# Attention with a bias on one core: pair 0's bias chunk moved, and pair 1's first head copied straight from PSUM

## The chip, the core and the metric

The kernel runs on one core of a Trainium2 chip. A core has five engines that run side by side, each with its own list of instructions in a fixed order: TensorE (PE: matmuls, and PEld: its weight loads), VectorE (DVE), ScalarE (ACT), GpSimd (POOL) and SyncE (SP). They wait for one another by semaphores. SP, ScalarE and POOL can issue DMA transfers; the transfers run on 16 shared DMA engines. The metric is the device time of one execution in microseconds (us); lower is better.

## The reference

Batch 4, 8 heads, sequence 1024, head size 64, all float32; the bias is one 1024x1024 matrix that all 32 heads share.

```python
scores = scale * np.matmul(q, k.transpose(0, 1, 3, 2))
scores = scores + bias
scores_max = np.max(scores, axis=-1, keepdims=True)
attn = np.exp(scores - scores_max) / (np.sum(np.exp(scores - scores_max), axis=-1, keepdims=True) + 1e-8)
return np.matmul(attn, v).astype(np.float32)
```

## The kernel before

Two heads make a pair; there are 16 pairs. The queries are cut into 8 chunks of 128. A **slot** is one chunk of one head: its scores against all 1024 keys, 128x1024 in float32, which is one of three PSUM places (`places`, each of two banks). There are 256 slots. Each is filled by PE (`fill`, 8 matmuls of 128 columns), turned into exp by ScalarE (`exp`, line 258, 128x1024 in one instruction) or, for 19 planned slots, by six steps on DVE, and then multiplied with v (`av`, line 312, 8 matmuls of 65 columns; the last column sums the row). DVE divides (`evac`) and SP stores.

The bias is not added anew for each head. A place starts with the bias by a matmul of the bias chunk with a scaled identity (`"b"`, line 241) and the scores of the first head on top (`"s"`, line 244). From then on the place keeps its PSUM: the next head's fill adds (new scores minus old scores), from one matmul of depth 128 whose two halves are the new head's k and q and the old head's k and negated q. So of each pair four arrays are needed: `ko`, `qo` (both heads of the pair stacked; q with a sign) and `ke`, `qe` (the pair's first head in rows 0 to 63, and the pair before's second head in rows 64 to 127). `copy_out` (lines 199, 201) brings the transposed k or q from PSUM to `ko` or `qo`; `double` (lines 210, 212) copies a half of them on into a `ke` or `qe`. Slots 0, 1, 2 are head 0 on query chunks 0, 1, 2 in places 0, 1, 2; slots 3 to 5 are head 1 there; slots 6 to 8 are head 2, pair 1's first; slots 9 to 11 head 3, and so on.

The order on each engine is set when the kernel is built. The opening (lines 337 to 392) is written out by hand: q and k of pair 0 are loaded in float32 on SP's queue (`q0f`, `k0f`), the bias's chunk 0 (`b0f`) on ScalarE's, and all are cast to bfloat16 by DVE and ScalarE (lines 370 to 373); ten matmuls of zeros keep PE running (line 360); ScalarE loads its exp table (line 347). All later loads go through POOL's queue, which casts on the way: bias chunks 1 and 2, then k and q of pair 1 (of q three chunks), k and q of pair 2, v of pair 0, k of pair 3, and so on (lines 352 to 358, then `early`). Behind the opening a planner (lines 394 to 826) with fixed costs and landing times decides the order: it appends to each engine's list the work that is ready first by its own clock. PE's transposes of k and q for later pairs (line 191, from the bfloat16 loads) go to the PSUM banks `xa` and `xb`, which are also those of `av`; a bank is free again when its copy has been made.

Of the kernel before, what the change touches and what calls it, by code (L numbers as in the profile page):

```python
# [16 lines left out]
def kernel(  # L17
# [13 lines left out]
    nc = tc.nc  # L31
# [150 lines left out]
    def transposes(pr, which, c0, n, tag, px=None):  # L182
        if px is None:
            px = ps_x.tile([P, n, P], BF, tag=tag, name="px")
        for c in range(n):
            if (pr, which, c0) in raws:
                nc.tensor.transpose(px[:, c, :], raws[pr, which, c0][:, c].rearrange("p t d -> p (t d)"), ident[:])  # L187
                continue

            for t in range(2):  # L190
                nc.tensor.transpose(px[t * D:(t + 1) * D, c, :], lands[pr, which, c0][:, t, c, :], ident[:],  # L191
                                    tile_position=(0, t * D))
        return px

    def copy_out(pr, which, c0, n, px):
        t = arrays(pr)
        cs = slice(c0, c0 + n)
        if which:
            nc.vector.tensor_copy(t["ko"][:, cs, :], px[:])  # L199
        else:  # L200
            nc.vector.tensor_scalar(t["qo"][:, cs, :], px[:], sgn[:], None, op0=ALU.mult)  # L201

    def double(pr, which, c0, n, part, w):
# [7 lines left out]
        else:  # L211
            w.tensor_scalar(to[("qe", "qe", "qs", "qz")[part]][rows, cs, :], t["qo"][rows, cs, :], -1.0, 1.0,
                            op0=ALU.mult, op1=ALU.mult)

    def negate(pr):

        t = (raws[pr, 0, 0] if 0 in BESIDE else lands[pr, 0, 0]).rearrange("p t c d -> p (t c d)").rearrange("p (c x) -> p c x", x=P)
        nc.vector.tensor_scalar(t, arrs[pr]["qo"][:], -1.0, 1.0, op0=ALU.mult, op1=ALU.mult)
        return t
# [10 lines left out]
            return t["ko"], t["qz"] if pr in first_pair else t["qs"]  # L230
        return (t["ko"], t["qo"]) if h % 2 else (t["ke"], t["qe"])

    def fill_half(s, b, what):

        x, c, h, start = slots[s]
        kk, qq = operands(s)
        for i in range(4):
            kc = 4 * b + i
            to = places[x][:, b, i * P:(i + 1) * P]
            if what == "b":  # L240
                nc.tensor.matmul(to, braw[:, c, :].rearrange("p (kp kc) -> p kc kp", kc=NCH)[:, kc, :], ident8[:],  # L241
                                 start=i == 0, stop=False, skip_group_check=True)
            else:
                nc.tensor.matmul(to, kk[:, kc, :], qq[:, c, :], start=False, stop=True, skip_group_check=True)  # L244

    def fill(s):
        for what in "bs" if slots[s][3] and s > 1 else "s":
            for b in range(2):
                fill_half(s, b, what)

    etile = {}

    def exp(s, i=0, n=2):

        if i == 0:
            etile[s] = ep.tile([P, NCH, P], BF, name="E")
        e = etile[s].rearrange("p (b c) q -> p b (c q)", b=2)
        nc.scalar.activation(e[:, i:i + n].rearrange("p b x -> p (b x)"),  # L258
                             places[slots[s][0]][:, i:i + n].rearrange("p b x -> p (b x)"), ACTF.Exp, scale=scale)
# [75 lines left out]
    with tc.manual_schedule():  # L335

        half = NCH // 2
        nc.sync.dma_start(out=q0f[:], in_=qf[0][:, :, :C0 * D].rearrange("p t (c d) -> p t c d", d=D))
        nc.scalar.dma_start(out=b0f[:], in_=bf_[:, 0, :])
        for i in range(2):  # L340
            nc.sync.dma_start(out=k0f[:, :, i * half:(i + 1) * half].rearrange("p t c d -> p t (c d)"),
                              in_=kf[0][:, :, i * half * D:(i + 1) * half * D])
# [2 lines left out]
        nc.vector.memset(sgn[:D, :], -1.0)  # L345
        nc.vector.memset(sgn[D:, :], 1.0)
        nc.scalar.activation(warm[:], warm[:], ACTF.Exp)
        make_identity(nc, ident[:])

        nc.gpsimd.memset(qz[0][D:, :, :], 0.0)  # L350
# [5 lines left out]
        load_k(2)  # L356
        load_q(2, slice(0, NCH))
        load_v(0)
        for i in range(10):
            nc.tensor.matmul(places[2][:, 0, :], zeros[:, :P], zeros, start=True, stop=True)  # L360

        cast = [de.tile([P, NCH, P], BF, name="de").rearrange("p c (t d) -> p c t d", d=D) for i in range(2)]
        qr0 = raws[0, 0, 0] = cast[0][:, half:half + C0]
# [5 lines left out]
        nc.vector.tensor_scalar(ident8[:], ident[:], 1.0 / scale, None, op0=ALU.mult)  # L369
        nc.vector.tensor_copy(qr0.rearrange("p c t d -> p t c d"), q0f[:])  # L370
        nc.vector.tensor_copy(kr0[0].rearrange("p c t d -> p t c d"), k0f[:, :, :half])
        nc.scalar.copy(braw[:, 0, :], b0f[:])
        nc.scalar.copy(kr0[1].rearrange("p c t d -> p t c d"), k0f[:, :, half:])

        pq = transposes(0, 0, 0, C0, "xa")
        pk = transposes(0, 1, 0, half, "xb")
        pk2 = places[2].bitcast(BF)[:, 1, :half * P].rearrange("p (c x) -> p c x", x=P)
        nc.vector.tensor_scalar(t0["qz"][:D, :C0, :], pq[:D], 1.0, None, op0=ALU.mult)
        copy_out(0, 1, 0, half, pk)
        for i in range(2):  # L380
            fill_half(0, i, "b")
        transposes(0, 1, half, half, None, px=pk2)
        copy_out(0, 1, half, half, pk2)
        copy_out(0, 0, 0, C0, pq)
        fill_half(0, 0, "s")
        exp(0, 0, 1)
        for i in range(2):
            fill_half(1, i, "b")
        fill_half(0, 1, "s")
        exp(0, 1, 1)  # L390
        double(0, 1, 0, NCH, 1, nc.vector)
        double(0, 0, 0, C0, 1, nc.vector)

# [38 lines left out]
        TR, SWITCH = 56, 190  # L432
        LATE, QCOST = 2, 4400
        flight = []

        LATE_LOADS = {"v5": 34200, "q0": 37900, "v6": 41000, "q1": 43000, "b3": 35900, "b4": 39300, "b5": 44400,
                      "b6": 46100, "b7": 47800}
# [82 lines left out]
                issue(0, E2, depth, load_b, pr)  # L520
                bias_at[pr] = LATE_LOADS["b%d" % pr]

        def doubles(pr, which, c0, n, t2, urgent):
            if not which and pr >= EARLY:
                def run(t3):
                    to = negate(pr)
                    last = parts(pr, 0)[-1]
                    for x in parts(pr, 0):
                        key = (("qe", "qe1", "qs", "qz")[x], pr + (x == 1), 0)
                        sp_q.append((t3 + 430 + L_DVE, lambda t4, x=x, key=key: copy(pr, x, key[0][:2], to, key, t4, x == last)))  # L530
                dve_q.append((t2, 0.2 if urgent else 2, 430, run))
                return
            for x in parts(pr, which):
                key = (("ke", "ke1")[x], pr + (x == 1)) if which else (("qe", "qe1", "qs", "qz")[x], pr + (x == 1), c0)
                if which and (pr >= EARLY or x == 1 and pr >= 2):
                    sp_q.append((t2 + L_DVE, lambda t3, x=x, key=key: copy(pr, x, "ke", arrs[pr]["ko"], key, t3)))
                elif which or urgent:
                    cost = (130 if which else 240) + 38 * n

                    def run(t3, x=x, key=key, cost=cost):  # L540
                        double(pr, which, c0, n, x, nc.vector)
                        ready[key] = t3 + cost + L_DVE
                    dve_q.append((t2, (0.2, 0.4, 0.4, 0.2)[x] if urgent else 2, cost, run))
                else:
                    double(pr, which, c0, n, x, nc.gpsimd)
                    pool(t2)
                    ready[key] = pool(0, 125 * n + 100) + 300
# [40 lines left out]
        def pe_cands():  # L588
# [69 lines left out]
            if pieces:  # L658
                pr, which, c0, n = pieces[0]
                need = need_at[pr, which, c0]  # L660
                ring = pr + linked(pr) - RING
                lag = len([s for s in avq[:NE] if s in e_at])
                if ((pr, which, c0) in raw_at and next_fill >= need - AHEAD and (ring < 0 or last_slot[ring] < next_fill)
                        and (lag < 4 or need - next_fill < 8)):
                    f, tag = min((x_free[y], y) for y in x_free)
                    r = max(f, raw_at[pr, which, c0])
                    cost = n * TR + SWITCH * (pr < EARLY or which not in BESIDE)
                    urgent = need - next_fill < 12
                    if r < 1e11:
                        def do(t, pr=pr, which=which, c0=c0, n=n, tag=tag, cost=cost):  # L670
                            x_free[tag] = 1e12
                            pieces.pop(0)
                            px = transposes(pr, which, c0, n, tag)
                            if pr < EARLY and which == 0 and c0 == 0:
                                freed(pr, t)

                            def run(t2):
                                copy_out(pr, which, c0, n, px)
                                done = t2 + 60 * n + (180 if which else 300)
                                x_free[tag] = done + L_DVE  # L680
                                if which:
                                    ready["ko", pr] = done + L_DVE
                                else:
                                    ready["qo", pr, c0] = done + L_DVE
                                doubles(pr, which, c0, n, done, urgent)
                            dve_q.append((t + cost + L_PE, 0 if urgent else 2, 60 * n + (180 if which else 300), run))
                        out.append((max(t_pe, r), cost, do, 2 if next_fill < need - 12 else 0.5, 0))
            return out

# [167 lines left out]
```

## Time and profile before

| what | us |
|---|---|
| median of 3 runs | 232.8 (232.72 to 233.51) |
| the profiled execution | 232.74 |
| its span | 230.8 |
| PE busy | 222.9 (97%) |
| ACT busy | 221.3 (96%) |
| DVE busy | 197.0 (85%) |
| POOL busy | 63.4 (27%) |
| exps on ScalarE (line 258) | 238, 218.1 in total, 1.124 each |
| first exp starts | 8.04 |

Times in the profile are us from the span's start. Busy time of PE counts a matmul from its issue to its modelled end, and matmuls overlap: 8 matmuls of 128 columns follow each other every 0.056 or so and each takes 0.219. Likewise the exps on ScalarE take 1.0 to 1.1 each, and start about 0.9 apart. An idle time in brackets is that of the engine just before the row, with what ended it. The chain of work that ended last is followed back from the last instruction, at each step to what released it or to the instruction ahead of it on its engine.

### The profile page before, as it was taken

To read this page: it belongs to the slowest core of one execution; us is meant where nothing else is said; L and a number is where in the kernel's file an instruction comes from. 1 tells how busy PE (TensorE), PEld (TensorE's weight loads), DVE (VectorE), ACT (ScalarE), POOL (GpSimd) and SP (SyncE) were. 2 spreads that over 40 slices of the span, in tenths; PEclk is the share of its full clock that TensorE was granted. 3 is DMA by queue.
4 is the path that set the end of the run, shared out by engine and by line. 5 is a ranking of instruction groups with operands and counts; after the bars stand their busy time and mean duration, and the time that the engine had idled before them with its cause. 6 is when DMAs were issued, how large, how long until landed. Compare 5 with 4: busy or idle time off the path is not lost.

```text
span 230.8 us, 10694 instructions
## 1 busy us (share of the span) xinstructions
PE 222.9 (97%) x4671; PEld 209.9 (91%) x4671; DVE 197.0 (85%) x294; ACT 221.3 (96%) x242; POOL 63.4 (27%) x115
## 2 busy tenths in 40 slices
PE   7999999999999999999999999999999999999993
PEld 2879999999999999998999999999998999999992
DVE  3595768799988997989889789899999899999993
ACT  3799999999999999999999999999999999999994
POOL 8816555144445374414216310000000000000000
PEclk9999999999999999999999999999999999999999
DMA  6999999969999799999999993111111112112212
GB/s 198 214 205 225 215 206 183 216 96 151 154 172 130 153 164 158 170 171 185 176 214 191 196 191 107 43 37 43 40 39 47 45 43 65 53 26 66 71 31 68
DMA packets 55645, 29.75 MB, mean 129 GB/s; under 512 B 31856, under 2 KB 51952, under 8 KB 55600
## 3 DMA queue, kind: packets, MB, share of 16 engines
q0 software_dynamic: 30336, 14.06, 49.6%
q1 hardware_dynamic: 24832, 14.43, 21.8%
q8 instruction: 36, 0.59, 1.1%
q10 hardware_dynamic: 432, 0.59, 0.9%
q14 instruction: 9, 0.07, 0.1%
HBM read 29.36 MB, written 8.39 MB: 164 GB/s over the span
## 4 chain that ended last, share of the span: by engine, by line
PE 43%; ACT 28%; issue 13%; DVE 5%; DMA 5%; POOL 3%; SPq 1%; DVEq 0%; ACTq 0%; POOLq 0%
ACT E L258 28%; PE pl L244 25%; PE po L312 12%; DMA k<-in_k_dram 4%; PE px L191 4%; PE pl L241 2%; DVE ob L322 1%; DVE dt L290 1%; DVE dy L275 1%; DVE de L295 1%; SPq L706 1%; POOL k L145 1%; POOL q L155 1%; DMA out_dram<-ob 1%; PE px L187 1%
## 5 line engine op out<-in xcount | busy, mean ns | idle before, releaser
L258 ACT ACTIVATE E<-pl 128x1024 bf16<-128x1024 f32 (+1 forms) x238 | 218.1, 1124 | 1.9 <-PE pl L244 1.7
L312 PE MATMUL po<-vall,E 128*128 128x65 bf16 x1896 | 92.0, 194 | 0.7 <-ACT E L258 0.7
L312 PEld LDWEIGHTS <-E 128*128 128x128 bf16 x1896 | 77.5, 98 | 1.8 <-ACT E L258 1.1
L244 PE MATMUL pl<-qo,ko 128*128 128x128 bf16 x1024 | 77.0, 219 | 1.2 <-ACT E L258 0.7
L244 PEld LDWEIGHTS <-ko 128*128 128x128 bf16 x1160 | 69.6, 98 | 4.4 <-issue 1.2
L244 PE MATMUL pl<-qe,ke 128*128 128x128 bf16 x888 | 66.0, 219 | 0.6
L244 PEld LDWEIGHTS <-ke 128*128 128x128 bf16 x888 | 53.4, 98 | 3.3
L275 DVE TENSOR_SCALAR dy<-pl 128x1024 int32<-128x1024 f32 x19 | 23.2, 1222 | 3.8 <-PE pl L244 2.7
L322 DVE TENSOR_TENSOR ob<-po,rs 128x448 f32<-128x448 f32 (+2 forms) x40 | 23.2, 581 | 2.0 <-DVE rs L320 0.5
L284 DVE SCALAR_TENSOR_TENSOR dt<-df 128x1024 f32<-128x1024 f32 x19 | 23.2, 1220 | 0.3
L295 DVE SCALAR_TENSOR_TENSOR de<-dy,dt 128x1024 uint16<-128x1024 int32 x19 | 23.2, 1219 | 0.1
L287 DVE SCALAR_TENSOR_TENSOR df<-dt,df 128x1024 f32<-128x1024 f32 x19 | 23.1, 1218 | 0.1
L290 DVE SCALAR_TENSOR_TENSOR dt<-df,dt 128x1024 f32<-128x1024 f32 x19 | 23.1, 1218 | 0.1
L138 POOL DMA_DIRECT2D q<-in_q_dram x18 | 16.8, 935 | 2.4 <-PE pl L244 1.4
L199 DVE COPY ko<-px 128x1024 bf16<-128x1024 bf16 (+1 forms) x16 | 10.7, 672 | 5.0 <-PE px L191 4.6
L201 DVE TENSOR_SCALAR qo<-px,sgn 128x1024 bf16<-128x1024 bf16 (+2 forms) x18 | 12.4, 686 | 2.5 <-PE px L187 1.7
L320 DVE RECIPROCAL rs<-po 128x7 f32<-128x7 f32 (+3 forms) x42 | 8.2, 194 | 7.1 <-PE po L312 6.8
L280 DVE TENSOR_SCALAR df<-dy 128x1024 f32<-128x1024 uint16 x19 | 13.0, 686 | 0.1
L165 POOL DMA_DIRECT2D v<-in_v_dram x16 | 11.3, 704 | 5.8 <-DVE rs L320 3.5
L473 POOL COPY tick<-q 1x1 bf16<-1x1 bf16 x12 | 3.9, 321 | 28.6 <-DMA q<-in_q_dram 28.6
L241 PE MATMUL pl<-ident,braw 128*128 128x128 bf16 x136 | 11.5, 227 | 0.1
L145 POOL DMA_DIRECT2D k<-in_k_dram x15 | 10.7, 710 | 2.6 <-issue 1.1
(55 smaller groups left out, 126.4 us busy)
## 6 DMA issues: line engine op xcount, KB each, us to landing
v<-in_v_dram POOLq DMA_DIRECT2D x16, 256.0 KB, 6.7
k<-in_k_dram POOLq DMA_DIRECT2D x15, 256.0 KB, 5.8
out_dram<-ob SPq DMA_DIRECT2D x35, 96.0 KB, 3.8
ke<-ko SPq DMA_DIRECT2D x22, 128.0 KB, 4.9
out_dram<-ob SPq DMA_DIRECT2D x40, 64.0 KB, 2.2
q<-in_q_dram POOLq DMA_DIRECT2D x18, 128.0 KB, 4.7
out_dram<-ob SPq DMA_DIRECT2D x68, 32.0 KB, 2.7
qe<-q SPq DMA_DIRECT2D x17, 128.0 KB, 4.6
```

The source lines that it names most:

```text
L138: nc.gpsimd.dma_start(out=t[:, :, y, :], in_=(qf, kf)[x][pr][:, y].rearrange("p (c d) -> p c d", d=D))
L145: nc.gpsimd.dma_start(out=t.rearrange("p t c d -> p t (c d)"), in_=kf[pr])
L241: nc.tensor.matmul(to, braw[:, c, :].rearrange("p (kp kc) -> p kc kp", kc=NCH)[:, kc, :], ident8[:], start=i == 0, stop=False, skip_group_ ...
L244: nc.tensor.matmul(to, kk[:, kc, :], qq[:, c, :], start=False, stop=True, skip_group_check=True)
L258: nc.scalar.activation(e[:, i:i + n].rearrange("p b x -> p (b x)"), places[slots[s][0]][:, i:i + n].rearrange("p b x -> p (b x)"), ACTF.Ex ...
L275: w.tensor_scalar(t["y"][:], places[slots[s][0]].rearrange("p b x -> p (b x)"), scale * LOG2E * 65536.0, 127.0 * 65536.0, op0=ALU.mult, op ...
L284: w.scalar_tensor_tensor(t["t"][:], t["f"][:], -G, t["f"][:], op0=ALU.add, op1=ALU.mult)
L287: w.scalar_tensor_tensor(t["f"][:], t["t"][:], Q, t["f"][:], op0=ALU.mult, op1=ALU.add)
L290: w.scalar_tensor_tensor(t["t"][:], t["f"][:], V, t["t"][:], op0=ALU.add, op1=ALU.mult)
L295: w.scalar_tensor_tensor(etile[s].bitcast(U16).rearrange("p c q -> p (c q)"), t["y"][:], 1.0 / 512.0, t["t"][:], op0=ALU.mult, op1=ALU.add)
L312: nc.tensor.matmul(po[:, j + i, :], etile[s][:, kc, :], vall[:, slots[s][2] % VR, kc, :], start=j + i + kc == 0, stop=kc == NCH - 1, skip_ ...
L322: nc.vector.tensor_tensor(ob[:, :n, :], po[:, :n, :D], rs[:, :n, :].to_broadcast([P, n, D]), op=ALU.mult)
```

## The change

Four edits, all for the first slots.

- The load of bias chunk 0 is issued on ScalarE's queue behind its table load and first small exp, not ahead of them. Its cast is split: columns 0 to 511 by ScalarE, behind the cast of k's second half, and columns 512 to 1023 by DVE.
- In slots 0, 1 and 2 the scores' matmuls come first and start the PSUM accumulation; the bias matmuls come behind and add. Slot 0's exp is one instruction over 1024 columns; it was two over 512, with matmuls of slots 0 and 1 between.
- Of the ten matmuls of zeros seven stay ahead of the transposes, and one each follows the transposes of q and of the first half of k.
- Pair 1's `ke` and `qe`, rows 0 to 63, are copied straight from the transposes in PSUM (`direct`), both ahead of the full copies to `ko` and `qo`. Before, they were copied from `ko` and `qo`.

```diff
+    def direct(pr, which, c0, n, px):
+        to = arrays(pr)["ke" if which else "qe"][:D, c0:c0 + n, :]
+        if which:
+            nc.vector.tensor_copy(to, px[:D])
+        else:
+            nc.vector.tensor_scalar(to, px[:D], 1.0, None, op0=ALU.mult)
...
-                                 start=i == 0, stop=False, skip_group_check=True)
+                                 start=first and i == 0, stop=not first, skip_group_check=True)
             else:
-                nc.tensor.matmul(to, kk[:, kc, :], qq[:, c, :], start=False, stop=True, skip_group_check=True)
+                nc.tensor.matmul(to, kk[:, kc, :], qq[:, c, :], start=first and i == 0, stop=not first, skip_group_check=True)
...
-        for what in "bs" if slots[s][3] and s > 1 else "s":
+        order = ("sb" if s < 3 else "bs") if slots[s][3] else "s"
+        for what in order:
             for b in range(2):
-                fill_half(s, b, what)
+                fill_half(s, b, what, len(order) > 1 and what == order[0])
...
-        nc.scalar.dma_start(out=b0f[:], in_=bf_[:, 0, :])
...
         nc.scalar.activation(warm[:], warm[:], ACTF.Exp)
+        nc.scalar.dma_start(out=b0f[:], in_=bf_[:, 0, :])
...
-        for i in range(10):
-            nc.tensor.matmul(places[2][:, 0, :], zeros[:, :P], zeros, start=True, stop=True)
+        keep_warm(7)
...
-        nc.scalar.copy(braw[:, 0, :], b0f[:])
         nc.scalar.copy(kr0[1].rearrange("p c t d -> p t c d"), k0f[:, :, half:])
+        nc.scalar.copy(braw[:, 0, :512], b0f[:, :512])
 
         pq = transposes(0, 0, 0, C0, "xa")
+        keep_warm(1)
         pk = transposes(0, 1, 0, half, "xb")
+        keep_warm(1)
         pk2 = places[2].bitcast(BF)[:, 1, :half * P].rearrange("p (c x) -> p c x", x=P)
+        transposes(0, 1, half, half, None, px=pk2)
         nc.vector.tensor_scalar(t0["qz"][:D, :C0, :], pq[:D], 1.0, None, op0=ALU.mult)
         copy_out(0, 1, 0, half, pk)
+        copy_out(0, 1, half, half, pk2)
+        nc.vector.tensor_copy(braw[:, 0, 512:], b0f[:, 512:])
+        copy_out(0, 0, 0, C0, pq)
         for i in range(2):
-            fill_half(0, i, "b")
-        transposes(0, 1, half, half, None, px=pk2)
-        copy_out(0, 1, half, half, pk2)
-        copy_out(0, 0, 0, C0, pq)
-        fill_half(0, 0, "s")
-        exp(0, 0, 1)
+            fill_half(0, i, "s", True)
         for i in range(2):
-            fill_half(1, i, "b")
-        fill_half(0, 1, "s")
-        exp(0, 1, 1)
+            fill_half(0, i, "b", False)
+        exp(0)
...
+            for x in [y for y in parts(pr, which) if y not in done]:
...
+                            early_pair = pr == 1 and c0 == 0
...
+                            def head(t2):
+                                direct(pr, which, c0, n, px)
+                                done = t2 + 60 * n + 180
+                                ready[("ke", 1) if which else ("qe", 1, 0)] = done + L_DVE
+                                behind.append((done, 0.1, copying, run))
+                                if len(behind) == 2:
+                                    dve_q.extend(behind)
```

In the built program, POOL's and SP's lists are the same in both kernels. ScalarE's differs in its first six instructions, DVE's and PE's in the order of the first 22 and 30 us; behind that they are the same.

## The prediction

> **What bounds the kernel now.** I read the chain that ended last first, over the whole run. Each row is start, length, what:
>
> ```profile
> 1.37 0.95 POOL qz L350
> ...
> 3.21 1.19 POOL braw L160 x2
> ...
> 7.95 9.14 DMA k<-in_k_dram
> 17.14 0.64 PE px L191 x16
> 17.78 0.55 PE pl L244 x8
> ...
> 48.22 0.46 PE pl L244 x8
> 48.76 0.66 ACT E L258
> ```
>
> The chain does not pass through the opening on SP, DVE and ScalarE that the change rewrites. It runs along POOL's queue of loads, into the landing of k of pair 3 at 17.09, and then only through PE until 48.76. Is PE really without a pause there? The table of stretches and PE's waits in 17 to 50 us answer:
>
> ```profile
> core 0: us, PE busy (x) PEld busy (x) DVE busy (x) ACT busy (x) POOL busy (x), PEclk, DMA share, GB/s
> 17.14:48.70 31.56, 31.39 (x691) 29.40 (x692) 22.59 (x48) 31.28 (x34) 14.91 (x34) 1.00 1.10 199
> ```
>
> ```profile
> PE px L191 <- DMA k<-in_k_dram: 0.4, 1, 0.4
> ```
>
> PE is busy 31.39 of 31.56 us and its one listed wait is that landing. Busy matmuls overlap, so that alone would not prove a full PE; that the chain steps from PE group to PE group without a gap does. DMA is full as well (share 1.10, 199 GB/s). Next ScalarE alone, to see what the opening is worth there:
>
> ```profile
> 5.25 1.04 ACT L372 CAST braw<-df 128x1024 bf16<-128x1024 f32 x1 [2.52 <-DMA df<-in_bias_dram]
> 6.71 0.62 ACT L373 CAST de<-dt 128x512 bf16<-128x512 f32 x1 [0.42 <-DMA dt<-in_k_dram]
> 8.04 0.60 ACT L258 ACTIVATE E<-pl 128x512 bf16<-128x512 f32 x1 [0.71 <-PE pl L244]
> 9.11 39.45 ACT L258 ACTIVATE E<-pl 128x512 bf16<-128x512 f32 x43 [0.47 <-PE pl L244]
> 48.76 23.94 ACT L258 ACTIVATE E<-pl 128x1024 bf16<-128x1024 f32 x26 [0.20 <-PE pl L244]
> ```
>
> From 9.11 ScalarE looks unbroken (exps of 1024 columns start 0.90 apart: 9.61, 10.51, 11.42 in the timeline), so an earlier first exp seems to be worth its full size. But at 48.76 ScalarE has to wait for PE, which by the chain counts from 17.14. An exp that starts earlier at 9 us makes this wait longer; it does not move 48.76. Last, PE just before the landing:
>
> ```profile
> 15.39 0.61 PE L244 MATMUL pl<-qo,ko 128*128 128x128 bf16 x8
> 16.18 0.61 PE L244 MATMUL pl<-qo,ko 128*128 128x128 bf16 x8 [0.17 <-ACT E L258]
> 17.14 0.64 PE L191 MATMUL px<-ident,k 128*64 128x128 bf16 x16 [0.35 <-DMA k<-in_k_dram]
> ```
>
> Slot 10 is filled about 16.7 (16.18 plus 8 matmuls, 0.45 to the next issue, 0.61 with the last one's latency); then PE stands still for 0.35. This idle time is where a faster opening goes.
>
> **The change part by part.** In the built orders, POOL's and SP's lists are the same in both kernels. ScalarE's differs in its first instructions only, DVE's and PE's in the first 22 and 30 us, and on PE the same slots stand before the transposes of pair 3's k.
>
> *Bias chunk 0 later, q and k of pair 0 earlier.* The issue on ScalarE's queue moves from 0.75 to behind the table load (1.28) and the warm exp (0.20): 2.25 at the latest. Before it landed 4.47 after its issue; with that it lands at 6.7, with the 2.9 of the quickest 128 KB copy at 5.2. I take 6.5, since all these loads together end as before (the last lands at 6.69) and this is now the last. q and k no longer share with 512 KB; at the 343 to 383 GB/s moved between 4.5 and 6.0 us those are 1.4 us. So q (5.42), k first half (5.98), k second half (6.69) land between 0 and 1.4 earlier; I take 1.2, as nearly all of the bias stood ahead: 4.2, 4.8, 5.5.
>
> *Slot 0.* ScalarE casts k's second half at 5.5 (0.62), PE transposes it (4, with latency about 0.4), DVE copies it (0.42): 6.95. DVE's half of the bias cast follows: 512 columns cost 0.43 in the row of k's first half; it ends at 7.4. ScalarE's half is 0.52 (half of 1.04) to 0.62 (k's row), so ends by 7.1. Eight bias matmuls, 0.66: exp(0) at 8.05, before 8.04. It is now one exp of 1024 instead of two halves with 0.47 idle between, so slot 1 may follow 0.905 later, at 8.95; its bias chunk lands at 7.95 (3.16 plus 4.79), and its matmuls end about 9.05. Slot 2's chunk lands at 9.17, its exp starts about 9.95, where it was 10.51. So ScalarE is 0.55 us earlier; with the other ends 1.0 earlier to 0.2 later.
>
> *Warm-up matmuls.* Three of ten leave the front, two return between transposes; 0.43 each (4.45 for 10), in time in which PE waits for q. Cost nothing; their cover is the loads' landing, and if that goes it is at most 0.9.
>
> *Pair 1's first head straight from PSUM.* DVE gains ke<-px, 64x1024: 0.42 (the same tile size from SBUF, L210) to 0.69 (same columns from PSUM, L199); I take 0.69. It gains qe<-px, 64x384: 0.35, L378's row, same size and source. It loses ke<-ko 0.42 and qe<-qo 0.25. With the bias half (0.43) DVE's opening grows by 0.80 us, into 2.04 us that it idled before 11.52. Slot 6 needed 0.69+0.42+0.40+0.25 = 1.76 of DVE, now 1.04. The full copies stand behind, and both PSUM banks stay taken for them: pair 2's transposes wait until about 13.2 instead of 12.80, and SP's copy of pair 2's k (14.20) is held behind its DVE copy by up to 0.75, landing at 20.1 instead of 19.39; its first reader is the fill at 23.74. Slot 9's operands, ready at about 13.6, are read at 15.39 before. Nothing here reaches PE's place at 17.14.
>
> *The meeting point.* By these steps PE ends slot 10 at about 16.1 (16.68 less 0.55) and waits for 17.09 all the same. Behind it stands the same PE work to 48.76. An opening up to 0.4 later would be free, an earlier one is not paid. What counts is only pair 3's k.
>
> *Its landing.* POOL's issues before it are the same, and its queue moves some 200 GB/s without a pause, so a shift at the front of that stream is passed on whole. Its first load took 4.79 from issue to landing; the quickest 256 KB load of the run 4.4. So it can land 0.4 earlier, if the hardware queues drain earlier in the new order. The other end: POOL's issues took 0.80 and 0.75 under DVE's casts, 0.70 to 0.73 otherwise; the casts now lie on the two bias issues, 0.1 each, so 0.2 later. I take 0.2 earlier, since q and k fill the engines that shared with the bias between 2.0 and 3.0 us (136 and 171 GB/s, against 316 and more later).
>
> **Sum.** The profiled execution took 232.74 (span 230.8 plus 1.94 around it), 0.06 under the median of 232.8. 232.74 - 0.2 = 232.5.
>
> **The rivals.**
> *The gain passes through.* If the landing moves with the opening, or PE has hidden slack, ScalarE's 0.55 to 1.0 is paid: about 232.74 - 0.8 = 231.9. For it speaks ScalarE's unbroken row; against it the chain, and that POOL's list is unchanged.
> *POOL's stream starts late (slower).* q's cast (0.55) and k's (0.43) move from 5.45 to about 4.2, towards the issues at 3.16 to 5.8. If a DVE cast stops POOL's descriptor writing outright, bias chunk 1 or pair 1's k comes up to 0.98 late, and so does all behind it, pair 3's k too; from 0.3 on it turns the sign. Price 0.7 in the middle: 233.4. Against it: under the same casts the issues grew by 0.1, not 0.5. The Trainium skill, "SBUF — State Buffer", "SBUF: two separate sides", states that rule: a DVE copy in a two-port mode locks GpSimd out of writing descriptors. By that rule this rival holds; the trace shows 0.80 against 0.70 at most.
> *The clock stays low.* Warm-up matmuls of 512 columns start 0.427 apart up to 5.02, transposes of 128 at 0.061 after 6.05: the clock rose in between. Seven in a row end at 4.2, the rest has holes. If it rises late, 27 matmuls to exp(0) and 32 for slots 1 and 2 cost 0.056 more each: up to 3.3 us, half of that if the clock rises midway, less the 1.0 that PE has to spare at 17.09 by my opening: 232.54 + 0.65 = 233.2, at worst 234.8. Against it: transposes and two fillers cover most of the hole. The Trainium skill, "TensorE: Matmul & The Clock Gate", "What's actually happening", puts the rise after a free-running window of some 3.4 us of activity. Seven matmuls fill 3.0 of it; no trace here shows where the window lies.
>
> **How the numbers follow.** Forecast (the landing pins it) 0.62, gain passes through 0.18, POOL late 0.12, clock 0.08. No change means within 0.5%, 1.16 us, about what a measurement can tell. The forecast and the first rival lie within it but for 0.06 (an opening over 1.1 earlier); of the last two about a third (the clock's worse half, a POOL delay over 1.4) goes over 233.96: 0.07. So faster 0.06, same 0.87, slower 0.07. The forecast's own range is 232.3 to 232.9; with half of the rivals on each side, 231.7 to 233.3.
>
> **What would show it.** Right: the bias issue near 2.2, q's cast near 4.2, slot 1's exp before 9.3, a longer wait of PE for pair 3's k (0.35 grows to about 0.8), its landing within 16.7 to 17.3, and the exp at 48.76 shifted as the landing is. Wrong: PE does not wait there; the exp at 48.76 comes earlier by more than the landing does; POOL's first issues longer than 0.9; transposes 0.1 apart after 6 us.

## The result and the profile after

The changed kernel took 234.88 us (median of 8 runs, 234.17 to 236.48); the kernel before, run beside it, 232.92 (8 runs, 232.35 to 233.51). The ratio is 1.0087 [1.0063, 1.0111]: slower by 0.9%, where 232.5 was forecast, and 233.3 as the upper end. The profiled execution took 234.71, with a span of 232.8 (before: 232.74 and 230.8). So 2.0 us are to be found in one pair of traces. Medians here and below leave out an execution that took over 1.5% more than the fastest of its kernel; there was one (237.05).

ScalarE's rows show where they arise. ScalarE's timeline of the changed kernel, from the start (start, length, what; in brackets the idle time before it):

```profile
0.75 1.28 ACT L356 ACT_TABLE_LOAD   x1 [0.75 <-PEq L870]
1.21 0.44 ACTq L358 DMA_DIRECT2D df<-in_bias_dram  x1
2.04 0.20 ACT L356 ACTIVATE warm<-warm 128x1 f32<-128x1 f32 x1
6.53 0.62 ACT L386 CAST de<-dt 128x512 bf16<-128x512 f32 x1 [4.29 <-DMA dt<-in_k_dram]
7.05 0.61 ACT L387 CAST braw<-df 128x512 bf16<-128x512 f32 x1
9.54 1.02 ACT L268 ACTIVATE E<-pl 128x1024 bf16<-128x1024 f32 x1 [1.87 <-PE pl L249]
11.24 1.02 ACT L268 ACTIVATE E<-pl 128x1024 bf16<-128x1024 f32 x1 [0.68 <-PE pl L249]
12.68 37.82 ACT L268 ACTIVATE E<-pl 128x1024 bf16<-128x1024 f32 x41 [0.41 <-PE pl L249]
50.71 23.94 ACT L268 ACTIVATE E<-pl 128x1024 bf16<-128x1024 f32 x26 [0.21 <-PE pl L252]
```

Slot 0's exp starts at 9.54, slot 1's at 11.24 (before 9.61), slot 2's at 12.68 (before 10.51, so 2.17 later). The exp that started at 48.76 before now starts at 50.71: 1.95 later. The last exp of the run is 2.06 later (228.26 against 226.20). The loss therefore stands by slot 2; behind that it changes by some tenths only. The rows also show the first step that went otherwise than forecast: the bias load was issued at 1.21, while the table load was still running.

Between slot 0 and slot 2 all exps wait for PE. The next fence is the table of stretches of the changed kernel; the column behind the POOL entry is the clock granted to TensorE.

```profile
core 0: us, PE busy (x) PEld busy (x) DVE busy (x) ACT busy (x) POOL busy (x), PEclk, DMA share, GB/s
5.33:8.74 3.41, 1.83 (x20) 1.18 (x21) 2.19 (x6) 1.14 (x2) 3.41 (x6) 1.00 1.13 234
8.74:12.15 3.41, 3.41 (x35) 3.41 (x34) 0.65 (x2) 1.93 (x2) 2.69 (x4) 0.50 1.27 196
```

From 8.74 to 12.15, which is exactly 3.413 us in the clock's records, TensorE had half its clock; from 5.33 to 8.74, and behind 12.15, it had all of it. (The records begin at 5.33. Ahead of that the zeros of 512 columns start 0.427 apart, at the full clock 0.216.) PE's timeline over the same place, with the sparse stretch ahead of it:

```profile
4.16 0.53 PE L187 MATMUL px<-ident,de 128*128 128x128 bf16 x3
4.48 0.63 PE L373 MATMUL pl<-E 128*128 128x512 bf16 x1
6.32 0.40 PE L187 MATMUL px<-ident,de 128*128 128x128 bf16 x4 [1.21 <-DVE de L385]
6.56 0.38 PE L373 MATMUL pl<-E 128*128 128x512 bf16 x1
7.20 0.40 PE L187 MATMUL pl<-ident,de 128*128 128x128 bf16 x4 [0.27 <-ACT de L386]
7.44 0.39 PE L252 MATMUL pl<-qz,ko 128*128 128x128 bf16 x4
8.12 0.40 PE L252 MATMUL pl<-qz,ko 128*128 128x128 bf16 x4 [0.30 <-DVE ko L199]
8.54 0.96 PE L249 MATMUL pl<-ident,braw 128*128 128x128 bf16 x8
9.29 1.06 PE L252 MATMUL pl<-qz,ko 128*128 128x128 bf16 x8
10.15 1.06 PE L249 MATMUL pl<-ident,braw 128*128 128x128 bf16 x8
11.00 1.06 PE L252 MATMUL pl<-qz,ko 128*128 128x128 bf16 x8
```

Groups of eight start 0.85 apart, which is 0.107 for each matmul of 128 columns; at the full clock they start 0.056 apart. 32 matmuls start in the half stretch (the table counts 35, with those that reach over its ends): 32 x 0.051 = 1.6 us, PE being full in it. Half of 3.413 us, 1.7, is the most that it can be. In the kernel before, the stretch of the same length that covers this place looks so (same columns):

```profile
5.78:9.19 3.41, 3.04 (x40) 2.48 (x41) 2.75 (x8) 1.80 (x4) 3.41 (x6) 1.00 1.15 223
```

Twice as many matmuls, and the clock stayed whole behind it. The Trainium skill, "TensorE: Matmul & The Clock Gate", "What's actually happening", says that the clock gate goes by how busy PE was in a free-running window of 3413 ns; the stretch of 3.413 us agrees with that.

The chain of the changed kernel, up to 52 us (start, length, what), no longer starts on POOL's queue:

```profile
1.75 4.76 DMA dt<-in_k_dram
6.53 0.63 ACT de L386
...
8.54 0.96 PE pl L249 x8
9.50 0.85 PE pl L252 x8
10.35 0.85 PE pl L249 x8
11.21 0.85 PE pl L252 x8
...
12.68 7.45 ACT E L268 x8
20.17 0.61 PE pl L252 x8
```

It goes from k's second half, on SP's queue, through the opening. At the forecast's meeting point, PE's timeline of the changed kernel:

```profile
17.59 1.35 PE L252 MATMUL pl<-qo,ko 128*128 128x128 bf16 x16
18.87 0.64 PE L191 MATMUL px<-ident,k 128*64 128x128 bf16 x16
```

PE transposes pair 3's k at 18.87, without waiting for it (before at 17.14; it is 1.73 late). The load itself landed at 16.28, 0.8 earlier than before; PE was not there to use it.

### The profile page after: what moved, and what is told of

It reads as the page before. It is cut to its first block, busy times and chain, and to the rows that moved or that the text cites. A ratio compares the mean times of both kernels' runs of the same rounds, so it can differ in the third digit from the quotient of the medians.

```text
span 232.8 us, 10695 instructions
## 1 busy us (share of the span) xinstructions
PE 224.0 (96%) x4670; PEld 211.4 (91%) x4670; DVE 197.7 (85%) x295; ACT 220.8 (95%) x241; POOL 65.8 (28%) x115
## 4 chain that ended last, share of the span: by engine, by line
PE 42%; ACT 33%; issue 14%; DVE 6%; DMA 3%; SPq 1%; DVEq 0%; ACTq 0%
ACT E L268 33%; PE pl L252 24%; PE po L322 11%; PE px L191 3%; PE pl L249 3%; DMA dt<-in_k_dram 2%; DVE ob L332 1%; DVE dt L300 1%; DVE dy L285 1%; DVE de L305 1%; SPq L735 1%; DMA out_dram<-ob 1%; PE px L187 1%; DVE df L290 1%; DVE df L297 0%
## 5 line engine op out<-in xcount | busy, mean ns | idle before, releaser
L268 ACT ACTIVATE E<-pl 128x1024 bf16<-128x1024 f32 x237 | 218.2, 1132 | 3.6 <-PE pl L249 3.0
L252 PEld LDWEIGHTS <-ko 128*128 128x128 bf16 x1160 | 70.4, 98 | 5.0 <-issue 1.4
L138 POOL DMA_DIRECT2D q<-in_q_dram x18 | 16.2, 904 | 3.2 <-PE pl L252 2.1
L488 POOL COPY tick<-q 1x1 bf16<-1x1 bf16 x12 | 6.1, 510 | 24.9 <-DMA q<-in_q_dram 24.9
L249 PE MATMUL pl<-ident,braw 128*128 128x128 bf16 x136 | 12.3, 238 | 0.1
```

Source lines behind the costliest of these rows:

```text
L138: nc.gpsimd.dma_start(out=t[:, :, y, :], in_=(qf, kf)[x][pr][:, y].rearrange("p (c d) -> p c d", d=D))
L252: nc.tensor.matmul(to, kk[:, kc, :], qq[:, c, :], start=first and i == 0, stop=not first, skip_group_check=True)
```

## The experiments

Edits are shown against the changed kernel unless another is named. "Half stretch" means that TensorE's mean granted clock over the execution was 0.993 or less: 3.413 us at half are 0.5 x 3.413 / 232.8 = 0.0073 of it. Profiled executions confirm that reading wherever there is one; the executions that were only timed have the mean alone, and none of them lies between 0.993 and 0.995. In the result's eight executions of the changed kernel six had a half stretch (median 234.88); the two without it took 234.54 and 235.45, so there it does not part slow from quick.

**Theory: the clock.** Too few matmuls stand in one 3.4 us stretch of the opening, and the next one is granted at half. Rivals: the new order of slots 0 to 2 with the split cast; the direct copies; the place of the bias load.

**Ten warm-up matmuls again.**

```diff
-        keep_warm(7)
+        keep_warm(10)
```

> The changed kernel with ten instead of seven matmuls of zeros ahead of the transposes; the two fillers stay. In the changed kernel the clock was full from 5.33 to 8.74 us, half from 8.74 to 12.15 and full again, and PE was busy for 1.83 of the 3.41 us before the half. Clock theory (PE idle too long in one stretch of 3.41 us halves the clock of the next): PE gains some 0.6 us of busy time in that stretch, 2.4 of 3.41; if that is enough there is no half stretch, slot 1's exp starts near 10.0 instead of 11.24, and the time is 232.4 to 233.3; if not, 234.9 as the changed kernel. Chain theory (the loads, casts and copies ahead of slot 0's exp became longer, whatever the clock): slot 0's exp at 9.5, 234.9. Pair 1 theory (the direct copies hold DVE and the PSUM banks): 234.9.

Measured: 233.71 (233.04 to 234.83), ratio to the kernel before 1.0032 [1.0004, 1.0059]; no half stretch in 10 executions. Slot 1's exp starts at 10.21, where it was 11.24. Three matmuls of zeros, which compute nothing, take the ratio from 1.0087 to 1.0032 (in two batches; side by side on one chip below).

**More fillers in the holes, the front left at seven.**

```diff
         pq = transposes(0, 0, 0, C0, "xa")
-        keep_warm(1)
+        keep_warm(4)
         pk = transposes(0, 1, 0, half, "xb")
-        keep_warm(1)
+        keep_warm(3)
...
             fill_half(0, i, "s", True)
+            if i == 0:
+                keep_warm(2)
```

> The changed kernel with the idle holes of PE filled: four matmuls of zeros instead of one behind q's transposes, three instead of one behind those of k's first half, two between the halves of slot 0's scores. Clock theory: PE is busy for about 3 of the 3.41 us, no half stretch, slot 1's exp near 10.0, 232.4 to 233.2. Chain theory: nothing is shorter, 234.9 or some tenths more. Pair 1 theory: 234.9.

Measured: 233.66, 1.0021 [0.9987, 1.0056]; no half stretch in 10. Slot 1 starts at 10.70: the fillers cost PE time of their own, and slot 1 still starts earlier than with a halved clock. It does not matter that the front has ten; it matters that PE is busy.

**No direct copies.**

```diff
-                            early_pair = pr == 1 and c0 == 0
+                            early_pair = False
```

> The changed kernel without the direct copies: pair 1's ke and qe are copied from ko and qo as before. Clock theory: the half stretch stays, 234.6 to 235.2. Pair 1 theory: 232.9. Chain theory: 234.9.

Measured: 234.82, 1.0057 [1.0011, 1.0103]; a half stretch in 5 of 8, among them the profiled one (8.33 to 11.74). Median with it 235.13, without 233.73. The direct copies are not what costs.

**The kernel before, with seven warm-up matmuls.** Against the kernel before:

```diff
-        for i in range(10):
+        for i in range(7):
```

> The kernel before with seven instead of ten matmuls of zeros, nothing else changed: PE stands idle from 4.2 to 6.05 us instead of from 5.45. Clock theory: a half stretch of 3.41 us in the opening, which meets 60 or so matmuls at 0.107 instead of 0.056: 233.8 to 235.3. Chain theory and pair 1 theory: 232.9, as the kernel before.

Measured: 233.78 (232.96 to 234.94), 1.0021 [0.9997, 1.0045]; a half stretch in 5 of 10, median 233.92 with and 233.47 without. Its table of stretches:

```profile
4.48:7.89 3.41, 1.90 (x24) 1.46 (x25) 1.70 (x5) 1.67 (x3) 3.41 (x5) 1.00 1.11 280
7.89:11.31 3.42, 3.42 (x33) 3.42 (x34) 1.13 (x4) 2.21 (x3) 2.78 (x5) 0.50 1.26 200
```

This edit alone, with none of the others, brings the half stretch about: in this profile the exp at 48.76 starts at 50.05, 1.3 later. But in half of the executions only, and the median moves too little to be told from none. So the warm-up can do it; it does not show that it does all of the 2.0.

**The bias load behind k, on SP's queue.**

```diff
                               in_=kf[0][:, :, i * half * D:(i + 1) * half * D])
+        nc.sync.dma_start(out=b0f[:], in_=bf_[:, 0, :])
...
-        nc.scalar.dma_start(out=b0f[:], in_=bf_[:, 0, :])
```

> The changed kernel (seven matmuls of zeros and two fillers) with the load of bias chunk 0 issued on SP's queue behind pair 0's k, so that it is really late; ScalarE's queue issued it at 1.21 in the changed kernel, beside its table load, and k landed at 5.82 and 6.51 as before. If the step that failed is the bias's place in time: k lands 0.8 to 1.2 earlier, near 4.8 and 5.5, the bias near 6.6, the hole of PE between 5.1 and 6.3 closes by itself, most executions have no half stretch, slot 1's exp starts near 9.0 to 9.4, and the time is 232.2 to 233.2. If k does not land earlier although the bias is behind it, the loads' landing is set by something else than sharing, the hole stays, 234.5 to 235.

Measured: 235.1, 1.0041 [1.0008, 1.0075]; half stretch in 5 of 10 (235.31 with, 234.13 without). k's first half landed at 4.14, but its second only at 7.05 and the bias at 8.30. This was to give k the early landing that the prediction had assumed; it moved one half.

**The kernel before with the moved load and the direct copies, nothing else.** Against the kernel before:

```diff
-        nc.scalar.dma_start(out=b0f[:], in_=bf_[:, 0, :])
...
         nc.scalar.activation(warm[:], warm[:], ACTF.Exp)
+        nc.scalar.dma_start(out=b0f[:], in_=bf_[:, 0, :])
...
-                                doubles(pr, which, c0, n, done, urgent)
+                                doubles(pr, which, c0, n, done, urgent, (0,) * early_pair)
+                            early_pair = pr == 1 and c0 == 0
```

> The kernel before (ten matmuls of zeros, bias matmuls first, slot 0's exp in two halves, the bias cast by ScalarE alone) with two parts of the change: the bias load behind the table load and warm exp in ScalarE's list, and pair 1's direct copies. If the new order of slots 0 to 2 and the split cast carry what the ten matmuls did not give back (0.3 to 0.8 us): this one is level with the kernel before, 232.6 to 233.4, slot 1's exp within 0.3 of 9.61. If the direct copies or the moved load carry it: 233.4 to 234.

Measured: 233.51, 0.9989 [0.996, 1.0019]; no half stretch in 10. ScalarE's timeline of it:

```profile
8.83 30.93 ACT L266 ACTIVATE E<-pl 128x512 bf16<-128x512 f32 x34 [0.47 <-PE pl L252]
40.05 8.49 ACT L266 ACTIVATE E<-pl 128x1024 bf16<-128x1024 f32 x9 [0.29 <-ACT E L266]
48.74 23.94 ACT L266 ACTIVATE E<-pl 128x1024 bf16<-128x1024 f32 x26 [0.20 <-PE pl L252]
```

Of these two parts of the change neither gain nor loss can be told. And the run answers a second question: the opening was 0.28 earlier (8.83 against 9.11), yet the exp of 48.76 came at 48.74. An earlier opening is not paid. That was the forecast's central step, and in this trace it holds. Pair 3's k landed at 16.83 there and PE took it up at 16.87, 0.27 earlier than before, which was not paid either; the chain then goes on through the loads of v on POOL's queue:

```profile
7.87 8.96 DMA k<-in_k_dram
16.89 0.38 POOL tick L482
17.27 6.93 DMA v<-in_v_dram
...
26.04 6.92 DMA v<-in_v_dram
```

So what pins this kernel, as far as one profile tells, is the stream of loads on that queue, and pair 3's k is only the first of them that PE meets.

**Ten zeros, the bias load first, no direct copies:** what is left is the order of slots 0 to 2, the split cast and the single exp.

```diff
+        nc.scalar.dma_start(out=b0f[:], in_=bf_[:, 0, :])
...
-        nc.scalar.dma_start(out=b0f[:], in_=bf_[:, 0, :])
...
-        keep_warm(7)
+        keep_warm(10)
...
-                            early_pair = pr == 1 and c0 == 0
+                            early_pair = False
```

> The changed kernel with ten matmuls of zeros, the bias load first on ScalarE's queue as before and no direct copies: what is left of the change is the order of slots 0 to 2, the split cast and the single exp. If these carry the rest: slot 1's exp at 10.0 to 10.3 instead of 9.61, 233.3 to 234, as with ten matmuls alone. If not: level with the kernel before, 232.6 to 233.3.

Measured: 234.22, 1.0025 [0.9994, 1.0057]; no half stretch in 10; slot 1 at 10.76. The interval holds no change as well as 1.3 us, so this run alone does not say what the order costs. (Its profiled execution has a pause of PE of 1.2 us between 20 and 50 us for which the trace names no wait.)

**The bias load held until k has landed.** All of the computation stays; the bias is only late.

```diff
-        nc.scalar.dma_start(out=b0f[:], in_=bf_[:, 0, :])
...
         nc.scalar.copy(kr0[1].rearrange("p c t d -> p t c d"), k0f[:, :, half:])
+        nc.scalar.copy(b0f[:, :1], k0f[:, 0, NCH - 1, D - 1:])
+        nc.scalar.dma_start(out=b0f[:], in_=bf_[:, 0, :])
```

> The changed kernel with the bias load issued only when pair 0's k has landed (ScalarE first copies one column of k into the bias tile, and the load waits for that): the bias shares with none of q and k. For the trace of the landings, not for the time, which the late bias must raise to 236 or more. If sharing with the bias set k's landing: k lands 0.8 to 1.2 earlier than in the changed kernel (5.82 and 6.51), near 4.8 and 5.5. If not: within 0.3 of those.

Measured: 241.42 (one execution). This is the price of the bias chunk by itself: issued at 6.06, it is there for the cast at 13.35 only, and slot 0's exp starts at 15.23. What the run was for is the time of k's two loads without the bias beside them. From issue to landing, in the changed kernel and then here:

```profile
DMA to landing us min/median/max: 4.6/4.7/4.8
```

```profile
DMA to landing us min/median/max: 2.9/3.2/3.5
```

So k can be 1.2 to 1.7 earlier, as the prediction took it: the second half at 5.30, the first at 4.12. It takes a bias load that is not beside them at all. PE, out of work after that, got two half stretches (10.85 to 17.68).

**The bias load issued at 2.27,** which is where the prediction had put it: the warm exp writes into the load's target, so the load waits for it.

```diff
-        nc.scalar.activation(warm[:], warm[:], ACTF.Exp)
+        nc.scalar.activation(b0f[:, :1], warm[:], ACTF.Exp)
```

> The changed kernel (seven matmuls of zeros, two fillers) with the small first exp written into the bias tile, so that the bias load has to wait for it: the issue comes at 2.3 to 2.5 us, as the prediction had assumed for the change, instead of 1.21. If the prediction's loads were right: k lands near 4.8 and 5.5, the hole of PE between 5.1 and 6.3 shrinks to less than 0.4, at most 2 in 10 executions have a half stretch, slot 1's exp near 9.2, 232.3 to 233.3 on a chip where the kernel before takes 232.9. If k lands as late as before: half stretches in about half of the executions, 234 to 235.

Measured: 235.01, 1.0086 [1.0052, 1.0119]; half stretch in 6 of 10 (236.16 with, 234.21 without). ScalarE's timeline of it:

```profile
2.27 0.38 ACTq L358 DMA_DIRECT2D df<-in_bias_dram  x1
7.72 0.62 ACT L386 CAST de<-dt 128x512 bf16<-128x512 f32 x1 [5.48 <-DMA dt<-in_k_dram]
```

The first half of k landed at 3.90. The second, issued at 1.75 and so 0.5 ahead of the bias, landed at 7.70, behind the bias (7.42). The forecast's landings of 4.2, 4.8 and 5.5 were not to be had by this edit even with the issue where the prediction saw it. PE's timeline of this run shows what that does to the hole:

```profile
8.39 0.55 PE L187 MATMUL pl<-ident,de 128*128 128x128 bf16 x4 [2.79 <-ACT de L386]
```

**The same with ten zeros.**

```diff
-        nc.scalar.activation(warm[:], warm[:], ACTF.Exp)
+        nc.scalar.activation(b0f[:, :1], warm[:], ACTF.Exp)
...
-        keep_warm(7)
+        keep_warm(10)
```

> As the run before it, with ten matmuls of zeros ahead of the transposes: no half stretch in any execution by the clock theory, wherever k lands. Level with the kernel before or up to 0.3% faster if k lands earlier; 0.2 to 0.4% slower, as with ten matmuls alone, if it does not.

Measured: 234.73 (9 executions), 1.0079 [1.0043, 1.0115]; half stretch in 3 of them (236.29 with, 234.38 without); k's second half at 7.85. Ten zeros are not a cure in themselves: with k as late as that the half stretch is in 3 of 9 executions instead of 6 of 10, and the median is lower by 0.3 only.

**The changed kernel again,** on the chip of the last three.

> The changed kernel once more, on the chip and beside the runs of the two before. Clock theory: in 4 to 8 of 10 executions the mean granted clock is 0.988 to 0.993 (a stretch of 3.41 us at half in the opening), and these are 1 to 1.7 us longer than the others; a median 1.2 to 2.2 above the kernel before. Chain theory: the executions are equally long whatever their clock.

Measured: 234.98 (5 runs), 1.0053 [1.0025, 1.008]; half stretch in 3 of 5 (235.16 with, 234.35 without). The profiled execution had none: slot 1's exp at 10.15, and PE at pair 3's k at 17.30, 0.16 later than before. The same kernel with a half stretch is there at 18.87 and, in the next run's profile, 18.56. One half stretch delays PE by 1.3 to 1.6 us there. The row without it:

```profile
17.30 0.64 PE L191 MATMUL px<-ident,k 128*64 128x128 bf16 x16
```

**Side by side on one chip:** the changed kernel, the same with ten zeros, and a kernel that also has the bias matmuls first again.

> The changed kernel as it is, on one chip with the next two. Split of its loss by the clock theory: executions with a half stretch in the opening (mean granted clock 0.993 or less) 0.6 to 1.7 us over those without; executions without one 0.4 to 1.4 over the kernel before, and level with the next run.

Measured: 235.61 (12 runs), 1.0070 [1.0040, 1.0100]; half stretch in 7 of 12 (235.86 with, 234.84 without).

```profile
4.37:7.78 3.41, 1.53 (x18) 0.87 (x15) 1.12 (x4) 1.12 (x2) 3.41 (x6) 1.00 1.09 279
7.78:11.20 3.42, 3.16 (x32) 2.90 (x29) 1.71 (x5) 1.04 (x2) 2.48 (x5) 0.50 1.25 198
```

The edit of the second is that of the first experiment, 7 to 10.

> The changed kernel with ten matmuls of zeros, beside the run before it. If the clock is about half of the loss: no half stretch in any execution, 0.4 to 1.0 us over the kernel before, 0.6 to 1.3 under the changed kernel. If the clock is nearly all of it: within 0.3 of the kernel before.

Measured: 233.80 (12 runs), 1.0014 [0.9988, 1.0040]; no half stretch in 12. Table of stretches and PE's timeline at the place of the hole:

```profile
5.20:8.62 3.42, 2.45 (x25) 1.34 (x23) 2.16 (x6) 1.14 (x2) 3.42 (x6) 1.00 1.12 239
```

```profile
6.27 0.40 PE L187 MATMUL px<-ident,de 128*128 128x128 bf16 x4 [0.39 <-DVE de L385]
...
8.48 0.68 PE L249 MATMUL pl<-ident,braw 128*128 128x128 bf16 x8
8.99 0.61 PE L252 MATMUL pl<-qz,ko 128*128 128x128 bf16 x8
```

The hole is 0.39 where it was 1.21, and the groups of slots 0 and 1 start 0.45 to 0.51 apart, not 0.85.

The third keeps ten zeros, the moved load, the split cast, slot 0's single exp and the direct copies:

```diff
-        order = ("sb" if s < 3 else "bs") if slots[s][3] else "s"
-        for what in order:
+        order = "bs" if slots[s][3] else "s"
+        for what in order[s == 1:]:
...
-        keep_warm(7)
+        keep_warm(10)
...
-        nc.scalar.copy(kr0[1].rearrange("p c t d -> p t c d"), k0f[:, :, half:])
+        nc.vector.tensor_copy(braw[:, 0, 512:], b0f[:, 512:])
         nc.scalar.copy(braw[:, 0, :512], b0f[:, :512])
+        nc.scalar.copy(kr0[1].rearrange("p c t d -> p t c d"), k0f[:, :, half:])
...
+        for i in range(2):
+            fill_half(0, i, "b", True)
         transposes(0, 1, half, half, None, px=pk2)
...
-        nc.vector.tensor_copy(braw[:, 0, 512:], b0f[:, 512:])
...
-        for i in range(2):
-            fill_half(0, i, "s", True)
-        for i in range(2):
-            fill_half(0, i, "b", False)
+        fill_half(0, 0, "s", False)
+        for i in range(2):
+            fill_half(1, i, "b", True)
+        fill_half(0, 1, "s", False)
         exp(0)
```

> The changed kernel with ten matmuls of zeros and the bias matmuls first again in slots 0 to 2 (slot 1's bias between the halves of slot 0's scores), with the casts of the bias ahead of the copies and of k's second half. Kept of the change: the moved load, the split cast, the single exp of slot 0, the direct copies. If the bias matmuls and casts behind the last copy of k carry the rest of the loss: slot 1's exp at 9.5 to 9.9 instead of 10.2, the time within 0.3 us of the kernel before. If the split cast, the load or the direct copies carry it: as with ten matmuls alone, 0.4 to 1.0 over.

Measured: 233.36 (12 runs, 232.53 to 234.14), 0.9987 [0.9962, 1.0012]; no half stretch in 12. ScalarE's timeline:

```profile
8.80 3.77 ACT L268 ACTIVATE E<-pl 128x1024 bf16<-128x1024 f32 x4 [1.70 <-PE pl L252]
```

Slot 0 starts at 8.80 (9.19 with the scores first and ten zeros), slot 1 at 9.73 (10.15). It is level with the kernel before, not ahead of it, and PE waits for pair 3's k again, for 0.39.

**What follows from all of them.** The half stretch was in 16 of 25 executions of the changed kernel, in none of the 64 of the six runs with ten zeros or with the fillers (leaving aside the one whose bias load was held to 2.27), and in 1 of 102 of the kernel before run beside the batches. Of the last batch's 2.0 us (235.61 against 233.60), 1.8 go with ten zeros in place of seven (233.80). So that the zeros cost this much is shown; that the half stretch carries all of it is not. In the traces it delays PE by 1.3 to 1.6 us, but executions of the changed kernel with it are above those without it by only 1.0 and 0.8 us in two batches (medians), and by nothing in the first. Bringing the bias to the front again takes a further 0.44 (233.36), but the two intervals overlap: slot 1's start, 0.42 earlier, is seen in the trace, its worth in time is not settled.

The changed kernel's executions *without* a half stretch are still some 1 us above the same kernel with ten zeros (234.84, five runs, against 233.80). In the two profiles the openings do not differ: slot 1's exp at 10.15 in both, pair 3's k at 17.30 and 17.29. The last exp is 0.84 later in the changed kernel (228.14 against 227.30), and what lies between are pauses of PE for which the trace names no wait: 0.81, 0.54 and 0.54, against 0.25 and 0.44. Such pauses (0.15 to 1.22) are in 12 of the 16 profiles, of quicker kernels too, and the profile of before has none. Each of the 17 of 0.15 or more behind 18 us ends 1.2 to 1.6 us after a 16 KB packet of the DMA queue of kind "instruction" has ended, of which there is one in 5.9 us; so PE was probably waiting for its next instructions. No run tests that, nor whether the changed kernel has more of these pauses than others; with five executions the 1 us may be chance, and this part stays open.

## Why the prediction was wrong, point by point

**The bias load: wrong.** "The issue on ScalarE's queue moves from 0.75 to behind the table load (1.28) and the warm exp (0.20): 2.25 at the latest." It moved to 1.21. The table load does not hold ScalarE's queue; the issue overtakes it and the warm exp. So the bias landed at 5.46 and not 6.5, and k at 5.82 and 6.51 and not 4.8 and 5.5: 0.17 earlier than before, where 1.2 was taken. Only q came much earlier (3.26, before 5.42; forecast 4.2). So q's transposes started early and the work behind them, which hangs on k, did not: the hole grew between the two. The prediction moved all three loads by one amount, as though the bytes ahead in the queues were all that counts.

**The warm-up matmuls: the step that failed.** "Cost nothing; their cover is the loads' landing, and if that goes it is at most 0.9." The cover was real, PE was waiting for loads in that time. But the cost of a matmul of zeros that is left out is not its own length: it is the share of a 3.41 us stretch that PE is busy. With seven zeros and k where it was, PE stood idle 1.21 and the next 32 matmuls ran at half the clock, 1.6 us. Side by side, the three zeros were worth 1.8 us (235.61 against 233.80), where the prediction had nothing and 0.9 at most. Whether seven would have been enough with k at 4.8 and 5.5 no run shows: the one run with seven that had both halves so early had its bias late. The price was there in the third rival, and its form was right (matmuls in the low clock times the 0.05 more each).

**The clock's rival: sized and weighed wrong.** It was given 0.08 and a middle of 233.2. It was worked out as a clock that rises late. In the trace the clock rose early (full from 5.33 on) and fell again. It was also credited with "the 1.0 that PE has to spare at 17.09 by my opening", made of 0.55 for the earlier opening and 0.4 for PE's own wait. The opening was not earlier, and only the 0.35 to 0.4 was there. With the 1.6 of the half stretch, the 0.54 that slot 1 is late with a whole clock too (10.15, before 9.61), and less PE's own wait of 0.35, the sum is 232.74 + 1.6 + 0.54 - 0.35 = 234.53; the profile has 234.71, and for the 0.2 between them there is no row. That the rival's worst case, 234.8, is so near to the result is luck: it was 3.3 for a clock that rises late, less a 1.0 to spare that was not there. "Against it: transposes and two fillers cover most of the hole" rested on k at 4.8: the chance hung on the first step, and the prediction did not say so.

**Slots 0 to 2: wrong by what has been said, and a little by the order.** Forecast 8.05, 9.05 and 9.95; measured 9.54, 11.24 and 12.68. With the clock whole and k as late as it was (ten zeros), slots 0 and 1 start at 9.19 and 10.15. The casts were sized right: DVE's half of the bias 0.42 (forecast 0.43), ScalarE's 0.61 (0.52 to 0.62).

**The direct copies: right.** DVE's timeline of the changed kernel:

```profile
13.70 0.68 DVE L219 COPY ke<-px 64x1024 bf16<-64x1024 bf16 x1 [4.29 <-PE px L191]
14.54 0.35 DVE L221 TENSOR_SCALAR qe<-px 64x384 bf16<-64x384 bf16 x1 [0.16 <-PE px L191]
```

0.68 and 0.35, where 0.69 and 0.35 were taken, and nothing of it reaches the end: with the moved load on the kernel before they change it by a ratio of 0.9989 [0.996, 1.0019].

**The meeting point: right on one side, and the side that mattered was the other.** "An opening up to 0.4 later would be free, an earlier one is not paid." The second half is shown by the run that opened 0.28 earlier. For the first, the profiled run with ten zeros and the scores first starts slot 1 0.54 later than the kernel before and reaches pair 3's k only 0.15 later, so some 0.4 were absorbed; its median is not told from the kernel before's (1.0014 [0.9988, 1.0040]). The change made PE 1.73 late, and 1.95 of lateness came out at 50.71. That "only pair 3's k" counts was too narrow (the stream of POOL's loads does), and its landing, 0.8 earlier against a forecast of 0.2, was of no use. A shift of 0.2 could not have been read from one trace anyway: in three profiles of the changed kernel that load landed at 16.28, 17.00 and 17.21.

**POOL's stream late: rightly small.** POOL's issues from 4.37 to 9.32 took 0.72 to 0.77 in the changed kernel (0.71 to 0.80 before), and the chance of 0.12 did not come true. The Trainium skill, "SBUF — State Buffer", "SBUF: two separate sides", says that a DVE operation in a two-port mode locks GpSimd out of writing descriptors; no such stall is seen here with DVE's casts beside these issues, and in which mode the casts ran no trace shows.

**The gain passes through: rightly refused,** by the same run that opened earlier. As it turned out, its chance of 0.18 belonged to the clock.

## What to carry to other kernels

Matmuls of zeros ahead of late loads are not to be costed at their own length, nor at nothing because PE waits anyway. Count what PE streams in each 3.4 us stretch once they are gone, with the landing times as they are and not as the change means them to be, and price a thin stretch at up to half a stretch of PE time in the next one (here 1.3 to 1.6 us of PE's time in the traces). When several steps hang on one forecast landing, the chance of the bad case is the chance that this landing is wrong.

## What the runs showed of the hardware

- **How busy is busy enough.** Take the matmuls of 128 columns that start in a stretch between two clock decisions at 0.056 each and those of 512 at 0.216, their spacing at the full clock, as a share of 3.41. The stretch behind was halved at 0.37 (19 and 1; the changed kernel, 5.33 to 8.74) and at 0.39 (24; the kernel before with seven zeros, 4.48 to 7.89). It was whole at 0.40 (7 and 4, and 0.12 us left of a fifth; ten zeros with the bias load held, 4.37 to 7.78), 0.43 (26; bias load behind k, 6.52 to 9.94), 0.44 (23 and 1; the changed kernel's profile without a half stretch, 5.49 to 8.90) and 0.66 (40; the kernel before, 5.78 to 9.19). In these six profiles the limit lies at about 0.4. No idle time was longer than 1.35 us in the two halved cases. The first recorded stretch begins at 4.37 to 6.88 us in the profiles, so one kernel falls on either side: 16 of 25.
- **A DMA issue overtakes ScalarE's table load.** Issued at 1.21, the table load running from 0.75 to 2.03. To be held, it had to depend on the warm exp's output; then it was issued at 2.27.
- **Loads on two queues don't land in the order of issue.** k's second half, issued 0.5 ahead of the bias, landed 0.28 behind it (7.70 and 7.42), 6.0 after its issue; without a bias load beside it, 3.5.
- **PE pauses behind code transfers.** 17 pauses of PE of 0.15 to 1.22 us, with no wait named, in 12 profiles, each ended 1.2 to 1.6 us after a 16 KB packet of the "instruction" queue (36 in a run) had ended. That is a coincidence in time, not an experiment.
